# Two sets of eviction buffers and an earlier history copy in the up-projection of a streaming encoder layer

## The chip, the cores and the metric

The kernel runs on one core of a Trainium2 chip. The metric is device time in microseconds of one execution. Three executions of the kernel before took 2345.95, 2350.46 and 2352.51 us; the median is 2350.46. A fourth execution was profiled; all rows shown are from it.

## The reference

One layer of a hybrid encoder runs over 2048 prompt tokens and 8 sample streams of 16 tokens (17 tiles of 128 tokens in all). A head mixer (mLSTM and sliding-window attention) and an output projection come first; their result, normalised, is h. Then the part that the change touches:

```python
def conv_ffn(h, conv_prev, w_up, w_conv, b_conv, w_down):
    T = h.shape[1]
    u = h @ w_up                                   # 1024 -> 2 * 2816
    ext = jnp.concatenate([conv_prev.astype(u.dtype), u], axis=1)
    c = b_conv + sum(ext[:, j:j + T] * w_conv[j] for j in range(CONV_W))   # CONV_W = 3, causal
    a, g = jnp.split(c, 2, axis=-1)
    return (jax.nn.silu(g) * a) @ w_down, ext[:, -(CONV_W - 1):]
```

The convolution needs the two rows of u before the first one of its stretch: its history. For the prompt it starts at zero and runs on from block to block of tokens; each sample stream brings its own two rows (`state_conv`). The last two rows are outputs too.

## The kernel before, in words

**Stages.** Input projection with the mixer woven into it, output projection, up-projection (`f_ups`, about 934 to 1876 us of the profiled span), down-projection (`f_downs`). The up-projection works on three blocks of tokens (`FBLOCKS`: 6, 6 and 5 tiles, that is 768, 768 and 640 columns; the sample tile is the last of the third block), and in each block on 22 units j. A unit is 128 value rows and 128 gate rows of u, all tokens of the block.

**A unit.** Value and gate, first and second half of the tokens make four quarters. They are computed with seven half-size products instead of eight, and combinations of weights and of tokens are prepared for that (the steps are numbered 1 to 7). Each product is 12 matmuls of 128 rows (`f_product`, L1875): inputs are split into a high and a low part (`split`: the cast of the high part on ACT is L220, the subtraction of the low part on DVE is L221) and three of the four part products are taken. The order in which products run is written by hand and is the only order that is fixed (`ORDER`; engine PE alone is scheduled by hand): for unit j products 6, 2, 5, then 1 of unit j+1, 3 of j, 7 of j+1, 4 of j. Units alternate between two sets of three PSUM banks A, B, C; B takes products 6, 5 and 3 one on top of the other, A takes 1 and 2, C takes 7 and 4.

**Evictions** (`f_after`) follow the products. After 1, ACT copies bank A to B (L1888). After 6, ACT copies B to the tile u2 (L1900). After 2, ACT copies A into the tile u (L1902). After 5, ACT copies B to the tile u4 (L1904) and DVE adds C and u4 into u (L1905, for the sample tile L1907). After 3, ACT copies B into u (L1909, L1911). After 4, DVE adds C and u2 into u (L1914). A later product that adds to a bank waits until the eviction before it has read the bank: product 5 for L1900, product 3 for L1904, product 4 for L1905 and L1907.

**Convolution.** After product 4 the history is put in: POOL copies two columns of `prev` to the front of u (L1915) and, in the third block, two columns of each sample stream from `sconv` into u (L1917). Then, for value and for gate, ACT computes the last tap with the bias into the tile cc (L1921) and DVE adds the two other taps (L1923, two instructions for each). POOL saves the last two columns of u for the next block (L1924) and for the outputs (L1926). The first block's cc go to DRAM (L1929) and are read back (L1938) beside the later blocks; the gate is ACT's L1945 and DVE's L1946 and L1947; its result goes out by L1948 and L1950.

**Buffers.** Tiles come from pools on the left or right side of SBUF. A tile with a tag and `bufs=n` rotates over n places; writing a place again waits until its last readers are done. Before, u, u2 and u4 have one place each, cc has two. `skew` allocates an unused tile so that the pool after it starts where wanted.

**Order.** On ACT, DVE, POOL and SP a planner places each instruction by its own estimate of when it can start; every engine then works through its list in order, and an instruction that has to wait holds up those behind it. SP issues the transfers in the same way: raw weights (L1777, L1779, L1781), prepared weights that were kept (L1808 reads, L1815 writes), and from the end of the up-projection on the down-projection's weights (L2010) and inputs (L1992). Weights are prepared 6 to 8 products ahead (`AHEAD`). When a block of tokens ends, the next block's combinations are made and split on ACT and DVE (`f_tokens`, L1753 to L1759 and the split's tiles hh and hl); that is the change of block.

Of the kernel before, what the change touches and what calls it, by code (L numbers as in the profile page):

```python
# [8 lines left out]
F32 = mybir.dt.float32  # L9
# [5 lines left out]
P = 128  # L15
# [3 lines left out]
DB = 8  # L19
# [185 lines left out]
class Prog:  # L205
# [23 lines left out]
    def run(self):  # L229
        PS = bass.MemoryType.PSUM  # L230
        nb = len(OBLOCKS)
        with ExitStack() as es:
            def enter(*a, **k):
                cm = self.pool(*a, **k)
                return cm.__enter__(), cm
            close = lambda cm: cm.__exit__(None, None, None)
            self.cp = es.enter_context(self.pool("const"))
            self.dp = es.enter_context(self.pool("dram", space=bass.MemoryType.DRAM))
            es.enter_context(self.tc.manual_schedule(engines={mybir.EngineType.PE}))
            self.setup()  # L240
            self.wp = es.enter_context(self.pool("wsb"))
            self.dps = es.enter_context(self.pool("dps", 3, PS))
            self.tp, tcm = enter("tsb", side="right")
            self.tps, tpcm = enter("tps", 5, PS)
            self.xp, xcm = enter("xsb")
            self.mp, mcm = enter("isb")
            chains = Chains(self)
            self.xs, self.gates, self.i_done = {}, {}, 0
            self.i_begin()
            self.warm_up()  # L250
            chains.weave(self.i_dense())
            close(mcm)
            wx, wxcm = enter("wx1sb")
            self.skew(wx, 64)
            self.unit_more(wx)
            self.mp, mcm = enter("osb")
            self.o_setup()
            for b in range(nb - 1):
                chains.weave(self.late_done(self.o_block(b)))
            chains.until(NPT - 1)  # L260
            chains.drain()
            close(tpcm)
            close(tcm)
            self.fp, fcm = enter("fsb", side="right")
            self.fup, fpcm = enter("fup", 3, PS)
            self.f_setup()
            dense = self.o_block(nb - 1)
            first = self.f_hT(0)
            next(first)
            n = 0  # L270
            for i, _ in enumerate(dense):
                if i >= 8:
                    next(first, None)
                if i == 21:
                    self.f_tokens(0, 1, "t1", "t3", 7, "t2", 6)

                if i >= 22 and n < (2, 4, 5)[min((i - 22) // 4, 2)]:
                    self.f_next()
                    n += 1
            for _ in first:  # L280
                pass
            assert not self.norms
            close(mcm)
            close(wxcm)
            close(xcm)

            self.wx, wxcm = enter("wx2sb")
            self.skew(self.wx, 64)
            self.f2, f2cm = enter("f2sb")
            self.f3, f3cm = enter("f3sb")  # L290
            self.f_ups(n)
            self.skew(self.f2, 480)
            self.skew(self.wx, 448)
            close(f3cm)
            close(f2cm)
            self.f2, f2cm = enter("dsb")
            self.f_downs()
            for cm in (f2cm, wxcm, fpcm, fcm):
                close(cm)
# [1577 lines left out]
    def f_after(self, b, j, s):  # L1877

        nc, f2 = self.nc, self.f2
        V, S = nc.vector, nc.scalar  # L1880
        W = len(FBLOCKS[b]) * P
        h = W // 2
        has_s = NPT in FBLOCKS[b]
        WP = W - P if has_s else W
        n = WP + (DB * (DS + 2) if has_s else 0)
        A, B, C = [x[:, :h] for x in self.banks[j % 2]]
        if s == 1:
            S.copy(B, A)  # L1888
            return
        if s == 7:  # L1890
            return
        if s == 6:
            u = f2.tile([P, 2, 770], F32, name="u", tag="u", bufs=1)
            self.u = u, *[f2.tile([P, 384], F32, name=m, tag=m, bufs=1)[:, :h] for m in ("u2", "u4")]
        u, u2, u4 = self.u
        us = u[:, :, 2 + WP:2 + n].rearrange("p v (b l) -> p v b l", b=DB) if has_s else None
        m = WP - h
        dec = lambda z: z[:, m:].rearrange("p (b l) -> p b l", b=DB)
        if s == 6:
            S.copy(u2, B)  # L1900
        elif s == 2:
            S.copy(u[:, 0, 2:2 + h], A)  # L1902
        elif s == 5:
            S.copy(u4, B)  # L1904
            V.tensor_add(u[:, 1, 2 + h:2 + WP], C[:, :m], u4[:, :m])  # L1905
            if has_s:
                V.tensor_add(us[:, 1, :, 2:], dec(C), dec(u4))  # L1907
        elif s == 3:
            S.copy(u[:, 0, 2 + h:2 + WP], B[:, :m])  # L1909
            if has_s:  # L1910
                S.copy(us[:, 0, :, 2:], dec(B))  # L1911
        if s != 4:
            return
        V.tensor_add(u[:, 1, 2:2 + h], C, u2)  # L1914
        nc.gpsimd.tensor_copy(u[:, :, 0:2], self.prev[:, :, j])  # L1915
        if has_s:
            nc.gpsimd.tensor_copy(us[:, :, :, 0:2], self.sconv[:, :, j])  # L1917
        c = self.f3.tile([P, 2, 768], F32, name="cc", tag="cc", bufs=2)[:, :, :n]
        for v in range(2):
            w = [self.cw[:, v * NFF + j, i:i + 1] for i in range(4)]  # L1920
            S.activation(c[:, v], u[:, v, 2:2 + n], AF.Identity, bias=w[3], scale=w[2])  # L1921
            for i in (1, 0):
                V.scalar_tensor_tensor(c[:, v], u[:, v, i:i + n], w[i], c[:, v], op0=ALU.mult, op1=ALU.add)  # L1923
        nc.gpsimd.tensor_copy(self.prev[:, :, j], u[:, :, WP:WP + 2])  # L1924
        if has_s:
            nc.gpsimd.tensor_copy(self.convs[:, :, j], us[:, :, :, DS:])  # L1926
        if b == 0:

            nc.sync.dma_start(self.zc[j], c)  # L1929
            return  # L1930
        self.f_gate(c, b, j, WP, n)

        i = (b - 1) * NFF + j
        i = i if i < 18 else i - 6 if 24 <= i < 28 else None
        if b and i is not None:
            W0 = len(FBLOCKS[0]) * P
            c = self.f3.tile([P, 2, 768], F32, name="cc", tag="cc", bufs=2)[:, :, :W0]
            nc.sync.dma_start(c, self.zc[i])  # L1938
            self.f_gate(c, 0, i, W0, W0)
# [231 lines left out]
```

## Time and profile before

| | |
|---|---|
| median of three executions | 2350.46 us |
| the profiled execution's own time | 2345.55 us |
| its span, from first to last instruction | 2343.8 us |
| busy in the span: PE (matmuls) | 2304.7 us |
| PEld (weight loads) | 2116.7 us |
| DVE | 1805.6 us |
| ACT | 1298.6 us |
| POOL | 244.7 us |
| mean granted clock of PE | 0.996 |

PE stands for TensorE's matmuls, PEld for its weight loads, DVE for VectorE, ACT for ScalarE, POOL for GpSimd, SP (with "q" for its queue) for the engine that issues transfers. A row of a timeline has its start, its duration, engine, line, operation, the tiles written and read, the shape, the count, and in brackets the idle time before it with what ended that. A row of waits has the waiting engine, tile and line, then who ended the wait, the total in us, how many times, and the longest. A row of windows has the window, its length, and the busy time and count of each engine, then the granted clock, the share of DMA engines busy, and GB/s.

### The profile page before, as it was taken

The numbers are of one execution on the slowest core, as the hardware profiler recorded it, in microseconds if no ns is written. First come the engines' busy times: TensorE is split into PE (matmuls) and PEld (weight loads), VectorE is DVE, ScalarE is ACT, GpSimd is POOL, SyncE is SP. The second block draws the span as 40 slices with busy tenths as digits, with TensorE's granted clock in tenths as the row PEclk, the third lists the DMA queues.
The fourth block names the chain that finished last, engine by engine and source line by source line (L and its number), as shares of the span: only waits on it lengthen the run. The fifth ranks groups of instructions, "written<-read, shape, count | busy, mean of one in ns | idle before, by whom it ended". The sixth has DMA issues, their size and how long they took to land.

```text
span 2343.8 us, 39880 instructions
## 1 busy us (share of the span) xinstructions
PE 2304.7 (98%) x14425; PEld 2116.7 (90%) x14425; DVE 1805.6 (77%) x3150; ACT 1298.6 (55%) x2465; POOL 244.7 (10%) x298
## 2 busy tenths in 40 slices
PE   8999999999999999999999999999999999999998
PEld 8989998999987777999999999999999978888887
DVE  8676586797688888987888777768766776796897
ACT  5353466676666665555556555545544544654653
POOL 0101101101112221300001000002000100000100
PEclk9999999999999999999999999999999999999999
DMA  8888889889877667787777889878988776756753
GB/s 277 285 306 287 290 280 319 283 280 340 296 256 246 215 206 268 269 323 275 279 270 252 309 314 320 303 272 264 316 289 261 241 278 212 237 193 222 238 184 108
DMA packets 297365, 624.98 MB, mean 267 GB/s; under 512 B 47052, under 2 KB 140240, under 8 KB 297168
## 3 DMA queue, kind: packets, MB, share of 16 engines
q1 hardware_dynamic: 296304, 619.29, 77.6%
q10 hardware_dynamic: 864, 3.15, 0.4%
q8 instruction: 114, 1.87, 0.3%
q14 instruction: 83, 0.68, 0.1%
HBM read 451.78 MB, written 170.56 MB: 266 GB/s over the span
## 4 chain that ended last, share of the span: by engine, by line
PE 72%; DVE 6%; DMA 2%; issue 2%; ACT 2%; POOL 0%; SPq 0%; DVEq 0%; ACTq 0%; POOLq 0%
PE fup L1875 18%; PE dps L1875 18%; PE dps L2079 6%; PE dps L734 6%; PE fup L2079 6%; PE fht L2079 5%; PE dps L225 2%; PE dps L227 2%; PE dps L226 2%; PE ppo L1370 1%; PE psc L1321 1%; PE ppt L1364 1%; PE dps L759 1%; DVE hl L221 1%; DVE w L221 1%
## 5 line engine op out<-in xcount | busy, mean ns | idle before, releaser
L1875 PE MATMUL dps<-hh,uw 128*128 128x384 f32 (+1 forms) x1848 | 480.6, 328 | 6.8 <-ACT u L1900 1.9
L1875 PE MATMUL fup<-hh,uw 128*128 128x384 f32 (+1 forms) x1848 | 479.4, 328 | 2.8 <-ACT u L1900 2.7
L1875 PEld LDWEIGHTS dps<-hh,uw 128*128 128x128 f32 x1848 | 329.7, 188 | 11.0 <-ACT u L1900 3.0
L1923 DVE SCALAR_TENSOR_TENSOR cc<-u,cw,cc 128x768 f32<-128x768 f32 (+1 forms) x264 | 252.4, 977 | 107.7 <-ACT cc L1921 105.5
L1875 PEld LDWEIGHTS fup<-hh,uw 128*128 128x128 f32 x1848 | 329.8, 188 | 4.3 <-ACT u L1900 3.8
L1875 PE MATMUL fup<-hl,uw 128*128 128x384 f32 (+1 forms) x924 | 302.4, 327 | 0.5 <-DVE hl L221 0.5
L1875 PE MATMUL dps<-hl,uw 128*128 128x384 f32 (+1 forms) x924 | 302.0, 327 | 0.0
L734 PE MATMUL dps<-w,oh 128*128 128x256 f32 x1344 | 258.0, 286 | 4.1 <-ACT zev L800 2.7
L221 DVE TENSOR_TENSOR w<-wraw,w 128x1024 fp32r<-128x1024 f32 (+2 forms) x163 | 188.1, 1159 | 61.7 <-ACT w L220 60.6
L220 ACT CAST w<-wraw 128x1024 fp32r<-128x1024 f32 (+2 forms) x163 | 160.9, 993 | 122.6 <-PE dps L734 56.1
L734 PEld LDWEIGHTS dps<-w,oh 128*128 128x128 f32 x1344 | 213.0, 190 | 16.3 <-issue 8.9
L220 ACT CAST uw<-wraw 128x1024 fp32r<-128x1024 f32 x126 | 122.8, 977 | 184.2 <-PE dps L2079 106.4
L1921 ACT ACTIVATE cc<-u,cw 128x768 f32<-128x768 f32 (+1 forms) x132 | 129.5, 997 | 122.2 <-DVE u L1914 61.1
L221 DVE TENSOR_TENSOR uw<-wraw,uw 128x1024 fp32r<-128x1024 f32 x126 | 142.4, 1131 | 67.7 <-ACT uw L220 67.1
L734 PE MATMUL dps<-w,ol 128*128 128x256 f32 x672 | 189.1, 281 | 0.0
L734 PE MATMUL dps<-oh,w 128*128 128x256 f32 x896 | 168.8, 284 | 7.0 <-ACT oh L579 2.2
L1875 PEld LDWEIGHTS fup<-hl,uw 128*128 128x128 f32 x924 | 173.4, 188 | 1.3 <-DVE hl L221 1.3
L2079 PE MATMUL fup<-uw,fu 128*128 128x512 f32 x726 | 172.1, 393 | 1.7 <-DVE uw L221 1.7
L1875 PEld LDWEIGHTS dps<-hl,uw 128*128 128x128 f32 x924 | 173.4, 188 | 0.0
L2079 PEld LDWEIGHTS fup<-uw,fu 128*128 128x128 f32 x726 | 136.2, 188 | 33.1 <-DVE uw L221 2.2
L2079 PE MATMUL dps<-uw,fu 128*128 128x512 f32 x660 | 163.2, 393 | 0.0
L734 PEld LDWEIGHTS dps<-oh,w 128*128 128x128 f32 x896 | 140.7, 189 | 13.8 <-issue 4.1
(337 smaller groups left out, 4624.4 us busy)
## 6 DMA issues: line engine op xcount, KB each, us to landing
uw<-zw SPq DMA_DIRECT2D x176, 512.0 KB, 5.0
zw<-uw SPq DMA_DIRECT2D x88, 512.0 KB, 2.9
w<-zws SPq DMA_DIRECT2D x72, 512.0 KB, 6.6
wv<-wup SPq DMA_DIRECT2D x66, 512.0 KB, 5.8
wraw<-wi SPq DMA_DIRECT2D x64, 512.0 KB, 5.1
wraw<-zt SPq DMA_DIRECT2D x60, 512.0 KB, 4.1
wraw<-wdn SPq DMA_DIRECT2D x45, 512.0 KB, 3.9
wraw<-wo SPq DMA_DIRECT2D x40, 512.0 KB, 4.9
```

Of the source, the lines that this page charges most:

```text
L220: nc.scalar.copy(hi, src)
L221: nc.vector.tensor_sub(lo, src, hi.bitcast(F32))
L225: mm(out, ah, bh, start=start, stop=False)
L226: mm(out, ah, bl, start=False, stop=False)
L227: mm(out, al, bh, start=False, stop=stop)
L734: mm(o, l, r, start=s in (1, 7) and c == k == i == 0, stop=k == 3 and i == 2, skip_group_check=True)
L759: mm(o, x, w, start=k == i == 0, stop=k == KD - 1 and i == 2, skip_group_check=True)
L1321: nc.tensor.matmul(ps[kvh][:, j, :nk], q[rs, j0 + j], k[rs, sel], start=i == 0, stop=i == 2)
L1875: mm(ps, l[:, k], r[:, k], start=s in (1, 7) and k == 0 and i == 0, stop=k == 3 and i == 2, skip_group_check=True)
L1921: S.activation(c[:, v], u[:, v, 2:2 + n], AF.Identity, bias=w[3], scale=w[2])
L1923: V.scalar_tensor_tensor(c[:, v], u[:, v, i:i + n], w[i], c[:, v], op0=ALU.mult, op1=ALU.add)
L2079: mm(ps, l[:, k, c], r[:, k], start=s in (1, 4, 7) and u == 0 and k == 0 and i == 0, stop=u == nu - 1 and k == n - 1 and i == 2, skip_grou ...
```

## The change

The tiles u, u2 and u4 get two places each (`bufs=2`). The history copies L1915 and L1917 are issued when the unit's tiles are taken, after product 6, and no longer after product 4; what they copy is the same. To make room, the scratch that is kept at the bottom of SBUF for transfers issued by POOL is set to 2048 bytes a partition; without the argument the program's constants begin at address 16384, with it at 2048, so all that is allocated from the left lies 14336 bytes lower. The padding after f2's pool is 448 bytes instead of 480, so that the pool behind it starts at the same place modulo 512. Lines behind the insertion have numbers up to 3 higher in the changed kernel (L1900, L1902, L1904, L1905 and L1914 become L1903, L1905, L1907, L1908 and L1917); L1915 and L1917 become L1895 and L1897; from L1918 on the numbers agree again. Line numbers in the prediction are those of before.

```diff
             self.f_ups(n)
-            self.skew(self.f2, 480)
+            self.skew(self.f2, 448)
             self.skew(self.wx, 448)
...
         if s == 6:
-            u = f2.tile([P, 2, 770], F32, name="u", tag="u", bufs=1)
-            self.u = u, *[f2.tile([P, 384], F32, name=m, tag=m, bufs=1)[:, :h] for m in ("u2", "u4")]
+            u = f2.tile([P, 2, 770], F32, name="u", tag="u", bufs=2)
+            self.u = u, *[f2.tile([P, 384], F32, name=m, tag=m, bufs=2)[:, :h] for m in ("u2", "u4")]
+            nc.gpsimd.tensor_copy(u[:, :, 0:2], self.prev[:, :, j])
+            if has_s:
+                nc.gpsimd.tensor_copy(u[:, :, 2 + WP:2 + n].rearrange("p v (b l) -> p v b l", b=DB)[:, :, :, 0:2], self.sconv[:, :, j])
...
         V.tensor_add(u[:, 1, 2:2 + h], C, u2)
-        nc.gpsimd.tensor_copy(u[:, :, 0:2], self.prev[:, :, j])
-        if has_s:
-            nc.gpsimd.tensor_copy(us[:, :, :, 0:2], self.sconv[:, :, j])
         c = self.f3.tile([P, 2, 768], F32, name="cc", tag="cc", bufs=2)[:, :, :n]
...
-    nc = bacc.Bacc("TRN2", target_bir_lowering=False, num_devices=1)
+    nc = bacc.Bacc("TRN2", target_bir_lowering=False, num_devices=1, dynamic_dma_scratch_size=2048)
```

## The prediction

> **What bounds the kernel now.** I read the page's busy shares first, then busy time in windows over the up-projection (about 934 to 1876 us), then what TensorE's weight loads and matmuls waited for there, then the timelines at the places found. The page:
>
> ```profile
> span 2343.8 us, 39880 instructions
> PE 2304.7 (98%) x14425; PEld 2116.7 (90%) x14425; DVE 1805.6 (77%) x3150; ACT 1298.6 (55%) x2465; POOL 244.7 (10%) x298
> ```
>
> TensorE is the bound: the whole program leaves its matmuls only 39 us of idle time. The windows below show where the up-projection's share lies; columns are the window, its length, then busy time and instruction count of PE, PEld, DVE, ACT, POOL.
>
> ```profile
> 1250.00:1280.00 30.00, 27.55 (x158) 26.91 (x157) 28.39 (x25) 20.20 (x26) 3.94 (x3) 1.00 0.68 231
> 1280.00:1580.00 300.00, 300.00 (x1737) 298.96 (x1737) 212.61 (x261) 154.53 (x252) 14.76 (x41) 1.00 0.87 303
> 1580.00:1610.00 30.00, 27.49 (x168) 26.93 (x168) 29.00 (x29) 19.57 (x28) 10.87 (x3) 1.00 0.66 210
> 1650.00:1660.00 10.00, 9.26 (x62) 8.84 (x61) 6.29 (x10) 4.70 (x9) 0.86 (x3) 1.00 0.90 298
> 1660.00:1855.00 195.00, 194.61 (x1322) 193.56 (x1322) 128.72 (x195) 96.98 (x191) 17.10 (x63) 1.00 0.88 280
> 1855.00:1880.00 25.00, 23.08 (x150) 21.75 (x149) 22.92 (x31) 17.40 (x28) 5.48 (x8) 1.00 0.62 187
> ```
>
> Inside a block of tokens (second row) PE does not stop at all. It stops where one block gives way to the next (first and third row), once at 1656, and at the end (last row). At the two changes of block DVE is busy 28.4 and 29.0 of 30 us. Who ended the stops, from 930 to 1925 us (total, times, longest):
>
> ```profile
> PEld fup L1875 <- ACT u L1900: 3.8, 4, 1.5
> PEld dps L1875 <- ACT u L1900: 3.0, 4, 1.6
> ...
> PEld dps L1875 <- DVE u L1905: 2.0, 1, 2.0
> PEld dps L1875 <- DVE u L1907: 1.5, 2, 1.1
> PEld dps L1875 <- ACT u L1904: 1.3, 3, 0.8
> PEld fup L1875 <- ACT u L1904: 0.5, 2, 0.4
> PE fup L1875 <- ACT u L1900: 2.7, 3, 1.2
> PE dps L1875 <- ACT u L1900: 1.9, 2, 1.3
> ```
>
> Four lines that evict quarters (L1900, L1904, L1905, L1907) hold PE up for 12.1 us by weight loads; L1900, the copy of bank B after product 6, is the largest with 6.8 (4.6 by matmuls). A stop costs something between its two views, so I take the mean of matmul idle and weight-load idle in a window. That bounds everything the change can reach: 2.8 + 2.8 + 0.95 + 0.9 + 2.6 = 10 us over the five windows with stops.
>
> **The change, part by part** (line numbers of before).
>
> *Two buffers for u, u2, u4.* No instruction is added or removed. What the single u holds back today is mostly not PE:
>
> ```profile
>   DVE cc L1923: 13.9, 12
>   ACT cc L1921: 40.9, 21
> ```
>
> The first row is L1902's idle time on ACT until the last convolution step of the unit before has read u: 1.2 us in each of 12 units. The second is who waited for L1917, the sample history's copy: L1921, in 21 of 22 units, 40.9 us of ACT. Both waits go (L1917 is dealt with below). Their worth on PE is zero inside a block, where PE is 300.00 of 300 busy; if that cover were gone the 54.8 us would be the price, which no window supports, since PE's whole idle time there is under 0.5 us per 195 or 300. What remains is the order in which ACT takes its work, and I went through the built order of both programs. PE's order is unchanged; ACT's, DVE's and SP's differ from the first change of block on.
>
> First change of block, ACT (start, duration):
>
> ```profile
> 1258.05 0.62 ACT L220 CAST uw<-wv 128x512 fp32r<-128x512 f32 x1 [3.55 <-PE dps L1875]
> 1258.58 1.48 ACT L220 CAST hh<-hraw 128x1536 fp32r<-128x1536 f32 x1
> 1259.96 1.02 ACT L1921 ACTIVATE cc<-u,cw 128x768 f32<-128x768 f32 x1
> 1260.89 0.45 ACT L1900 COPY u<-dps 128x384 f32<-128x384 f32 x1
> 1274.25 0.63 ACT L220 CAST uw<-wv 128x512 fp32r<-128x512 f32 x1
> 1276.01 1.03 ACT L1921 ACTIVATE cc<-u,cw 128x768 f32<-128x768 f32 x1 [1.13 <-DVE u L1914]
> 1276.95 0.46 ACT L1900 COPY u<-fup 128x384 f32<-128x384 f32 x1
> ```
>
> L1900 stands behind the old unit's second L1921, which waits for DVE (L1914, 1.13 us at the second place). With a second u2 it needs only product 6, and the changed order has it ahead of all three rows: possible from about 1258.05 instead of 1260.89, and from 1274.25 instead of 1276.95. Both leads (2.8 and 2.7 us) exceed the longest stop (1.6), so both stops go: 30 minus 27.55 is 2.45, 30 minus 26.91 is 3.09, mean **-2.8 us**. Next to be late is DVE: 1.6 us of its 30 are idle there, and the casts of tokens moved behind L1900 come 0.45 us later each time. If DVE ends the stops instead, this term is nearer 0; I take all of it because the stops now end with ACT, not DVE.
>
> Second change of block: 2.51 and 3.07, mean 2.8. Of it L1905 has 2.0 by weight loads and DVE's order at L1905 is the same after; that stays. The rest is L1900, again moved ahead of L1921: **-0.9 us**.
>
> At 1656 ACT itself waits for a transfer:
>
> ```profile
> 1653.96 1.76 ACT L1921 ACTIVATE cc<-u,cw 128x656 f32<-128x656 f32 x2 [3.23 <-DMA zf<-cc]
> 1655.63 0.40 ACT L1900 COPY u<-fup 128x320 f32<-128x320 f32 x1
> ```
>
> L1900 stays behind both L1921 there, and cc keeps its two buffers. The stop is 0.74 to 1.16; a gate (L1945) that moves one cast forward may bring that transfer forward. I take a third: **-0.3 us**.
>
> Inside the third block (0.39 to 1.44 idle, mean 0.9) the stops belong to L1904 and L1907, and a unit there looks like this:
>
> ```profile
> 1737.39 0.27 ACT L1911 COPY u<-fup 128x128 f32<-128x128 f32 x1
> 1738.93 0.62 ACT L220 CAST uw<-wv 128x512 fp32r<-128x512 f32 x1 [1.27 <-PE dps L1875]
> 1741.50 1.76 ACT L1921 ACTIVATE cc<-u,cw 128x656 f32<-128x656 f32 x2 [1.95 <-POOL u L1917]
> 1743.16 0.40 ACT L1900 COPY u<-dps 128x320 f32<-128x320 f32 x1
> 1740.70 0.49 DVE L1914 TENSOR_TENSOR u<-fup,u 128x320 f32<-128x320 f32 x1 [0.42 <-PE fup L1875]
> ```
>
> *The history's copies moved to the unit's beginning.* 66 copies L1915 and 22 copies L1917 stay on POOL, one place earlier, no DMA among them. L1915 of a unit now goes ahead of the save L1924 of the unit before, and waits for the same last L1923 two units back as today; L1924 queues behind it, and only the same unit's L1915 in the next block and u's release wait for L1924, a unit or more later: 0 us. L1917 no longer waits for L1914, so the value half of L1921 can run at 1737.7 instead of 1741.5. DVE then takes two L1923 before L1914, which goes back by about 0.3 us; the gate half ends, and L1900 with it, about 0.6 us sooner; L1945 and L1904 behind it gain more. The window's **-0.9 us** goes.
>
> The last window has 1.92 to 3.25 idle, mean 2.6. By the same laying out of queues L1900 comes 0.5 us sooner, but L1904 now stands behind the down-projection's cast of a weight group and L1945; I take **-0.6 us**.
>
> *Scratch and paddings.* Scratch for POOL's own DMAs shrinks, so everything allocated from the left moves down 14336 bytes; nearly all left-hand tiles keep their address modulo 512. POOL issues no DMA: every queue of the page is hardware or instruction. u2, u4 and one u move by 32 bytes modulo 64. L1902 (u) and L1900 (u2) are now 32 apart and take 463 and 459 ns at the median:
>
> ```profile
> L1902 ACT COPY u<-fup x33: 407/463/489, 943.4 to 1857.3; 128x384 f32<-128x384 f32 x22, 128x320 f32<-128x320 f32 x11
> L1900 ACT COPY u<-fup x33: 401/459/484, 942.5 to 1854.0; 128x384 f32<-128x384 f32 x22, 128x320 f32<-128x320 f32 x11
> ```
>
> 4 ns times 264 copies is 1 us on ACT, beside PE: 0.
>
> **Sum**: -2.8 - 0.9 - 0.3 - 0.9 - 0.6 = -5.5 us, between 0 and -10. The profiled execution took 2345.55 us, 4.9 below the median 2350.46 of the three runs; the mean of all four is 2348.6. I put the sum on that mean: **2343 us**, 7.4 below the median.
>
> **The rivals.** (1) *All stops at evictions go*: -10 us, also L1905's, because ACT hands it u4 sooner. Against it: DVE is 29.0 of 30 busy there. 2338.6. (2) *Nothing reaches PE*: DVE becomes the releaser at both changes of block; for it, its 1.0 to 1.6 us of idle time; against it, that L1900 is the named releaser. 2348.6. (3) *POOL gets in DVE's way.* The sample copies take 212 ns at the median but up to 1141:
>
> ```profile
> L1917 POOL COPY u<-sconv x22: 212/214/1141, 1615.5 to 1875.9; 128x32 f32<-128x32 f32 x22
> L1915 POOL COPY u<-prev x66: 188/494/12615, 937.4 to 1870.2; 128x4 f32<-128x4 f32 x66
> ```
>
> and L1915 from 188 to 12615, so POOL is held back while DVE works. Moved beside L1915, the 22 copies meet a working DVE. Charged in full, 22 times 0.214 is 4.7 us: 2347.8. DVE has 66 of 195 us idle in that block, so I take 0. The Trainium skill ("SBUF — State Buffer", section Who interferes with whom) says that a DVE instruction with two SBUF inputs and a GpSimd read exclude each other for a whole instruction and whoever starts first wins; the stretched L1915 agrees, and the rule speaks against the move. By the rule with POOL always first the sum would be -0.8, by the rows -5.5.
>
> (4) *Slower: a raw weight load falls behind in SP's queue.* In the third block the built order puts the load of wv behind one more L1808, which waits for PE:
>
> ```profile
> 1740.30 0.33 SPq L1777 DMA_DIRECT2D wv<-wup  x1
> 1751.24 0.62 ACT L220 CAST uw<-wv 128x512 fp32r<-128x512 f32 x1 [1.27 <-PE fup L1875]
> wv<-wup SPq DMA_DIRECT2D x15, 512.0 KB, 5.9
> SPq L1808 <- PE dps L1875: 100.1, 57, 3.8
> ```
>
> It is issued at 1740.30, lands 5.9 later at 1746.2, and the next cast from a wv is at 1751.24: 5.0 us in hand at least, against one wait of at most 3.8. If two waits add, a unit is late by up to 2.6; over 20 units 52 us, 2395 at worst. It decides from 0.6 us a unit (12.5 us, 2355.6); since each unit's load could catch up I price it there.
>
> **How the numbers follow.** 0.3% of the median is 7 us, about what a measurement of this kernel can tell from no change: under 2343.4 is faster. Forecast 0.62, its own range 2338 to 2348, split 0.33 faster and 0.29 same; rival 1 0.12 (faster); rival 2 0.08 and rival 3 0.04 (same); rival 4 0.14 (slower). Together 0.45, 0.41, 0.14. The range goes from all of it on the lowest run (2345.55 - 10 = 2335.5, and 1 below) to rival 4's point of decision, a little under: 2334.5 to 2355.
>
> **What would show it.** Right: in 1250 to 1280 PE's idle time falls from 2.45 to under 0.5 and L1900 as releaser from 6.8 to under 3; L1902 no longer waits for L1923, nor L1921 for POOL; PE's and DVE's busy times stay. Wrong: L1923, hl or L1905 in L1900's place with equal totals (rival 2), a longer L1923 in the third block (rival 3), or L220 waiting for wv's transfer in many units (rival 4). A change before 930 us, where every engine's order is unchanged, would mean that addresses matter, which no row here prices.

## The result, and the profile after

The changed kernel takes 2344.69 us at the median of 20 executions (2340.11 to 2350.57); the kernel before, beside it, takes 2349.06 us (2344.25 to 2355.42). The ratio is 0.9982 with a 95% interval of 0.9975 to 0.9989: 4.2 us less (2.6 to 5.9). That is inside the 0.3% that the prediction called no change, and on the side it forecast. The time, 1.7 us above the 2343 of the forecast, came out of parts that were not those of the forecast. The rest is about that. In the experiments below one of the 12 executions of e3_hist took 10117 us and one of the 12 of e9_load11 9955 us; the medians given there count them, the ratios leave them out.

The page of the changed kernel, its two first lines:

```profile
span 2340.1 us, 39886 instructions
PE 2301.8 (98%) x14425; PEld 2115.6 (90%) x14425; DVE 1806.9 (77%) x3150; ACT 1302.5 (56%) x2465; POOL 249.6 (11%) x298
```

The work is the same on every engine, and TensorE (PE) is still the bound. The windows that the prediction looked at, now of the changed kernel, with the beginning of the down-projection as a seventh; the columns are the window, its length, busy time and count of PE, PEld, DVE, ACT and POOL, granted clock, DMA share, GB/s:

```profile
1250.00:1280.00 30.00, 29.20 (x169) 28.88 (x168) 28.41 (x25) 20.69 (x27) 10.24 (x3) 1.00 0.70 233
1280.00:1580.00 300.00, 300.00 (x1737) 299.28 (x1736) 213.67 (x262) 156.45 (x253) 16.30 (x42) 1.00 0.88 305
1580.00:1610.00 30.00, 28.26 (x178) 27.96 (x177) 29.73 (x33) 20.08 (x30) 11.81 (x7) 1.00 0.68 212
1650.00:1660.00 10.00, 10.00 (x71) 10.00 (x70) 7.39 (x12) 5.41 (x11) 1.34 (x4) 1.00 0.94 288
1660.00:1855.00 195.00, 190.72 (x1296) 189.67 (x1296) 129.08 (x191) 98.54 (x188) 17.29 (x62) 1.00 0.88 279
1855.00:1880.00 25.00, 23.89 (x155) 22.75 (x155) 22.84 (x31) 18.01 (x30) 2.44 (x6) 1.00 0.62 193
1880.00:1925.00 45.00, 45.00 (x197) 36.51 (x196) 34.80 (x39) 19.26 (x25) 0.00 (x0) 1.00 0.86 310
```

The last of these windows in the kernel before, which the prediction did not show:

```profile
1880.00:1925.00 45.00, 43.26 (x189) 34.94 (x188) 33.43 (x37) 19.36 (x25) 0.00 (x0) 1.00 0.87 315
```

PE's idle time falls from 2.45 to 0.80 us at the first change of block, from 2.51 to 1.74 at the second, from 0.74 to 0 at 1656. In the third block (fifth row) it rises from 0.39 to 4.28. In the down-projection, of which the prediction says nothing, 1.74 us go.

Who ended the stops of PE in the changed kernel, from 930 to 1925 us (waits of PE: total, times, longest):

```profile
PE dps L1875 <- ACT u L1907: 2.8, 2, 1.7
PE dps L1875 <- DVE u L1908: 2.5, 2, 1.7
PE fup L1875 <- DVE hl L221: 1.5, 2, 1.2
PE fup L1875 <- ACT u L1903: 1.3, 1, 1.3
PE dps L1875 <- ACT uw L220: 1.4, 2, 0.7
PE dps L1875 <- ACT u L1903: 1.3, 2, 1.0
```

L1903, the copy of bank B after product 6 (L1900 before), is down from 4.6 to 2.6 us. What is left of it and the larger stop of L1907 are all in the third block or at the end, where the kernel before had 1.3 us in two stops of the one and 0.5 us in one of the other.

Windows cut a stage at fixed times. To compare executions I took the start of the first matmul of certain products from each trace, and the differences between them. The change of block runs from product 1 of unit 21 of the old block to product 7 of unit 1 of the new one; "units 3 to 8" from product 7 of unit 3 to product 7 of unit 9; the first unit ends where its product 5 begins. The changed kernel was profiled twice. All in us:

| stretch | before | after | after, second profile |
|---|---|---|---|
| all ahead of the up-projection | 933.95 | 933.25 | 931.03 |
| first unit | 9.71 | 10.71 | 10.61 |
| rest of the first block | 303.76 | 303.45 | 303.64 |
| first change of block | 36.39 | 34.48 | 34.46 |
| second block | 293.24 | 293.10 | 293.89 |
| second change of block | 34.17 | 33.12 | 33.11 |
| units 1 to 2 of the third block | 24.62 | 24.62 | 24.62 |
| units 3 to 8 | 76.51 | 79.21 | 78.46 |
| units 9 to 19 | 135.42 | 135.42 | 135.42 |
| end of the up-projection | 27.50 | 26.18 | 26.18 |
| down-projection | 468.49 | 466.54 | 466.54 |

Five rows carry the change: -1.9, -1.05, +2.7 (+1.95 in the second profile), -1.3 and -1.95. Their sum is -3.5 (-4.3), and the time changed by -4.2. The first two rows of the table and the second block vary between executions of one program: by 3.9, 1.0 and 0.9 us between the two profiles of e2_bufs below.

### The profile page after: what moved, and what is told of

Same layout as the page of the kernel before. It is cut to its first block, busy times and chain, and to the rows that moved or that the text cites. A ratio compares the mean times of both kernels' runs of the same rounds, so it can differ in the third digit from the quotient of the medians.

```text
span 2340.1 us, 39886 instructions
## 1 busy us (share of the span) xinstructions
PE 2301.8 (98%) x14425; PEld 2115.6 (90%) x14425; DVE 1806.9 (77%) x3150; ACT 1302.5 (56%) x2465; POOL 249.6 (11%) x298
## 5 line engine op out<-in xcount | busy, mean ns | idle before, releaser
L1923 DVE SCALAR_TENSOR_TENSOR cc<-u,cw,cc 128x768 f32<-128x768 f32 (+1 forms) x264 | 257.7, 978 | 124.0 <-ACT cc L1921 105.4
L221 DVE TENSOR_TENSOR w<-wraw,w 128x1024 fp32r<-128x1024 f32 (+2 forms) x163 | 187.8, 1157 | 59.3 <-ACT w L220 58.2
L220 ACT CAST w<-wraw 128x1024 fp32r<-128x1024 f32 (+2 forms) x163 | 161.0, 993 | 122.3 <-PE dps L734 63.8
L220 ACT CAST uw<-wraw 128x1024 fp32r<-128x1024 f32 x126 | 122.7, 977 | 180.8 <-PE dps L2079 106.4
L1921 ACT ACTIVATE cc<-u,cw 128x768 f32<-128x768 f32 (+1 forms) x132 | 131.9, 999 | 118.2 <-DVE u L1917 96.4
L221 DVE TENSOR_TENSOR uw<-wraw,uw 128x1024 fp32r<-128x1024 f32 x126 | 142.6, 1132 | 68.1 <-ACT uw L220 67.7
```

Source lines behind the costliest of these rows:

```text
L220: nc.scalar.copy(hi, src)
L221: nc.vector.tensor_sub(lo, src, hi.bitcast(F32))
```

## The experiments

Theory at this point: the buffers give the two changes of block; something about transfers costs the third block; the down-projection gains by accident of an order. Rivals: the lower addresses do it (scratch); the history's move does it all; the third block's loss is rival 4's late weight load.

**Placement alone, buffers alone, history alone, and a third cc.** The first four kernels split the change into its parts, and add one buffer to it. Edits are against the changed kernel unless it is said otherwise, and each ratio is to executions of the kernel before taken beside that kernel's.

e1_space, the kernel before with the smaller scratch and nothing else:

```diff
-    nc = bacc.Bacc("TRN2", target_bir_lowering=False, num_devices=1)
+    nc = bacc.Bacc("TRN2", target_bir_lowering=False, num_devices=1, dynamic_dma_scratch_size=2048)
```

> Placement alone: the kernel before with the scratch at 2048 bytes, everything on the left 14336 bytes lower, every engine's order as before. If placement carries part of the gain (theory P): ratio 0.9985 or less, and the stop of 1.7 us at 1918 us goes here too. If it is the buffers' doing (theory B): ratio 1.000 within 0.07%, idle time of PE in 1250 to 1280 stays at 2.4 us and in 1580 to 1610 at 2.5, and what differs outside the up-projection is chance.

Measured: 2348.3 us, ratio 0.9996 (0.9985 to 1.0006). The stretches of the table are those of before (36.39, 34.18, 76.03, 27.51, 468.49; the 0.5 us at units 3 to 8 is within what two profiles of one program differ by there). No effect of the addresses is seen, as the prediction took it.

e2_bufs, the buffers with the history where it was:

```diff
             u = f2.tile([P, 2, 770], F32, name="u", tag="u", bufs=2)
             self.u = u, *[f2.tile([P, 384], F32, name=m, tag=m, bufs=2)[:, :h] for m in ("u2", "u4")]
-            nc.gpsimd.tensor_copy(u[:, :, 0:2], self.prev[:, :, j])
-            if has_s:
-                nc.gpsimd.tensor_copy(u[:, :, 2 + WP:2 + n].rearrange("p v (b l) -> p v b l", b=DB)[:, :, :, 0:2], self.sconv[:, :, j])
...
         V.tensor_add(u[:, 1, 2:2 + h], C, u2)
+        nc.gpsimd.tensor_copy(u[:, :, 0:2], self.prev[:, :, j])
+        if has_s:
+            nc.gpsimd.tensor_copy(us[:, :, :, 0:2], self.sconv[:, :, j])
```

> Two buffers each, history still copied after product 4. Theory B (the second buffers let the planner put L1900 ahead of L1921 at the changes of block): PE's idle time falls to about 0.8 in 1250 to 1280 and 1.7 in 1580 to 1610 as in the changed kernel. Theory H (the earlier history copy moves the third block's convolution forward, into transfers of cc that have not landed, and costs the 4 us in units 5 to 8): no such stops here, PE idle in 1660 to 1855 at 0.4 to 1, so ratio 0.9965 to 0.998, lower than the full change's 0.9982. If H is wrong and the buffers make those stops: idle about 4 there, ratio about 0.998 or above.

Measured: 2341.69 us, ratio 0.9971 (0.9960 to 0.9983). The changes of block take 34.51 and 33.12, as after; units 3 to 8 take 76.91 (76.92 in a second profile), as before; the end of the up-projection 26.62; the down-projection 468.50, as before. So the buffers give the whole of both changes of block. Its interval overlaps the changed kernel's; which of the two is faster is not settled by that. These stretches add up to 3.3 us under before, a little less than the 4.0 us at which the interval begins; no profile shows where more could come from.

e3_hist, the history moved with one buffer each:

```diff
-            self.skew(self.f2, 448)
+            self.skew(self.f2, 480)
...
-            u = f2.tile([P, 2, 770], F32, name="u", tag="u", bufs=2)
-            self.u = u, *[f2.tile([P, 384], F32, name=m, tag=m, bufs=2)[:, :h] for m in ("u2", "u4")]
+            u = f2.tile([P, 2, 770], F32, name="u", tag="u", bufs=1)
+            self.u = u, *[f2.tile([P, 384], F32, name=m, tag=m, bufs=1)[:, :h] for m in ("u2", "u4")]
```

> One buffer each, history copied when the unit begins. Theory B: PE idle in 1250 to 1280 and 1580 to 1610 as before (2.4 and 2.5). Theory H: L1921 no longer waits for L1917 and the stops in units 5 to 8 of the third block appear, 2 to 4 us in 1660 to 1855; ratio 0.9995 to 1.0015. If the history's move is what helps: ratio 0.998 to 0.999.

Measured: 2344.41 us, ratio 0.9983 (0.9972 to 0.9994). The changes of block are those of before (36.41, 34.18), units 3 to 8 take 76.82, the end 26.49, the down-projection 466.52, as after. The history's move gives the down-projection's 1.95 us, which no part of the prediction touches. Neither part alone costs the third block anything that shows beside the 76.0 to 77.4 us of the kernels with the order of before (e1 and e9 below); together they do. The theory H of these two expectations, that the history's move brings the loss by itself, fails with that.

e4_cc3, the changed kernel with three buffers for cc:

```diff
-        c = self.f3.tile([P, 2, 768], F32, name="cc", tag="cc", bufs=2)[:, :, :n]
+        c = self.f3.tile([P, 2, 768], F32, name="cc", tag="cc", bufs=3)[:, :, :n]
...
-            c = self.f3.tile([P, 2, 768], F32, name="cc", tag="cc", bufs=2)[:, :, :W0]
+            c = self.f3.tile([P, 2, 768], F32, name="cc", tag="cc", bufs=3)[:, :, :W0]
...
-    nc = bacc.Bacc("TRN2", target_bir_lowering=False, num_devices=1, dynamic_dma_scratch_size=2048)
+    nc = bacc.Bacc("TRN2", target_bir_lowering=False, num_devices=1, dynamic_dma_scratch_size=1024)
```

> The changed kernel with three buffers for cc (scratch 1024 for the room). Theory H (units 5 to 8 stop because ACT waits for cc's transfers): PE idle in 1660 to 1855 falls from 4.3 to under 1, L1921 no longer waits for the store of zf, ratio 0.996 to 0.997 (4 us under the changed kernel). If the raw weights' load in SP's queue is what stops those units: idle stays at 2 or more and L220 still waits for wv; ratio 0.998.

Measured: 2339.86 us (six executions, 2338.82 to 2342.38), ratio 0.9960 (0.9945 to 0.9974): faster than both kernels. Units 3 to 8 fall from 79.21 to 74.31, 2.2 under before; every other stretch is the changed kernel's.

What the third cc takes away is seen in the ACT timeline. First the changed kernel in unit 5 of the third block (start, duration, then the row; in brackets the idle time before it and who ended it):

```profile
1657.25 0.85 ACT L1945 ACTIVATE th<-cc 128x768 f32<-128x768 f32 x1 [1.07 <-DMA cc<-zc]
...
1661.33 0.94 ACT L1921 ACTIVATE cc<-u,cw 128x656 f32<-128x656 f32 x1 [2.34 <-DMA zf<-cc]
1662.17 0.60 ACT L220 CAST uw<-wv 128x512 fp32r<-128x512 f32 x1
1664.25 0.94 ACT L1921 ACTIVATE cc<-u,cw 128x656 f32<-128x656 f32 x1 [1.47 <-DVE u L1917]
1665.09 0.41 ACT L1903 COPY u<-dps 128x320 f32<-128x320 f32 x1
```

Then the same unit with three cc:

```profile
1657.53 0.85 ACT L1945 ACTIVATE th<-cc 128x768 f32<-128x768 f32 x1 [0.73 <-DVE cc L1947]
...
1660.46 0.94 ACT L1921 ACTIVATE cc<-u,cw 128x656 f32<-128x656 f32 x1
1661.65 0.62 ACT L220 CAST uw<-wv 128x512 fp32r<-128x512 f32 x1 [0.25 <-PE dps L1875]
1664.31 0.94 ACT L1921 ACTIVATE cc<-u,cw 128x656 f32<-128x656 f32 x1 [2.04 <-DVE u L1917]
1665.17 0.43 ACT L1903 COPY u<-dps 128x320 f32<-128x320 f32 x1
```

ACT works through its list in order. With two cc, L1921 waits until a convolution result has left for memory (zf<-cc), L1945 until a convolution result of the first block has come back from it (cc<-zc); with three, neither waits for a transfer, and PE's stops at L1903 go. The waits of ACT for these transfers from 1640 to 1720 us, in the changed kernel:

```profile
ACT cc L1921 <- DMA zf<-cc: 6.2, 4, 2.4
ACT th L1945 <- DMA cc<-zc: 4.0, 3, 1.7
ACT uw L220 <- DMA wv<-wup: 2.5, 2, 2.2
```

and with three cc the one row of that kind that is left:

```profile
ACT uw L220 <- DMA wv<-wup: 2.9, 3, 1.5
```

The third row of the changed kernel is rival 4's wait for a raw weight load. It remains with three cc at 2.9 us, and units 3 to 8 take 74.31 us there, with one stop of 0.2 us. So rival 4's wait is there, and is not what costs the time; the kernel before has more of it (4.0 us in 2 from 1640 to 1760 us).

**Which buffer, whose cc, which gates.** e5_u2u4_only is the changed kernel with one u; e6_u_only has one u2 and one u4.

```diff
-            self.skew(self.f2, 448)
+            self.skew(self.f2, 480)
...
-            u = f2.tile([P, 2, 770], F32, name="u", tag="u", bufs=2)
+            u = f2.tile([P, 2, 770], F32, name="u", tag="u", bufs=1)
```

> The changed kernel with one buffer for u, and two each for u2 and u4 as in the change. Theory A (the prediction's: the copy of bank B waits for the old unit's u2, so a second u2 is what lets it go ahead): the first change of block takes 34.5 us as after (before 36.4), the second 33.1 (before 34.2), and the time is that of the changed kernel, 2342 to 2346. Rival B (the copies of bank A into u are what holds the order; u2 comes along behind): 36.4 and 34.2 as before, and 2345 to 2348. In both the down-projection keeps the 466.5 us of the changed kernel, since the history is copied early.

```diff
-            self.u = u, *[f2.tile([P, 384], F32, name=m, tag=m, bufs=2)[:, :h] for m in ("u2", "u4")]
+            self.u = u, *[f2.tile([P, 384], F32, name=m, tag=m, bufs=1)[:, :h] for m in ("u2", "u4")]
```

> The changed kernel with two buffers for u alone, and one each for u2 and u4. Theory A (a second u2 is what counts): both changes of block as before the change, 36.4 and 34.2 us, and 2345 to 2348. Rival B (a second u counts): 34.5 and 33.1, and 2342 to 2346. If each does part of it, the first change lies between at about 35.5.

Measured: e5 2342.81 us, 0.9975 (0.9962 to 0.9988), changes of block 34.51 and 33.12, units 3 to 8 78.30. e6 2347.11 us, 0.9997 (0.9986 to 1.0008), changes of block 38.72 and 34.17, units 3 to 8 76.53. Waits of PE from 1250 to 1300 us, e5:

```profile
PE dps L1875 <- DVE u L1908: 0.8, 1, 0.8
```

and e6:

```profile
PE fup L1875 <- ACT u L1903: 1.9, 1, 1.9
PE dps L1875 <- ACT u L1903: 1.3, 1, 1.3
```

Theory A holds: u2 and u4 are what lets L1903 go ahead, and the larger tile u needs no second place. (0.8 of e6's 38.72 is a longer stop; the other 1.6 are a dip of the clock, below.) The 13.9 us that ACT waited for L1923 before, which a second u was to remove, were indeed worth nothing. The third block's loss goes with u2 and u4 too: both kernels copy the history early, and only e5 has most of the loss.

e7_cc3_alone, the third cc in the kernel before (edit against that kernel, with the smaller scratch for room, as in e1):

```diff
-        c = self.f3.tile([P, 2, 768], F32, name="cc", tag="cc", bufs=2)[:, :, :n]
+        c = self.f3.tile([P, 2, 768], F32, name="cc", tag="cc", bufs=3)[:, :, :n]
...
-            c = self.f3.tile([P, 2, 768], F32, name="cc", tag="cc", bufs=2)[:, :, :W0]
+            c = self.f3.tile([P, 2, 768], F32, name="cc", tag="cc", bufs=3)[:, :, :W0]
```

> The kernel before with a third buffer for cc, and nothing of the change. Theory A (ScalarE waits for transfers of cc in the third block whatever the change does, and the change only brings more work behind these waits): units 3 to 8 of the third block take about 74.3 us (before 76.5, after 79.2); the changes of block stay 36.4 and 34.2, the down-projection 468.5; time about 2 us under before, 2346 to 2348. Rival B (the third buffer helps only together with the change): units 3 to 8 stay at 76.5, and 2348 to 2351.

Measured: 2347.18 us, ratio 0.9989 (0.9973 to 1.0005); units 3 to 8 at 74.43, all else as before (36.42, 34.17, 468.48). The transfers held PE up in the kernel before too, by 2.1 us; the change made that 4.8 (with three cc 74.4, with two 76.5 before and 79.2 after).

e8_gates_later, the changed kernel with the four read-backs that fell into units 2 to 5 of the third block done in units 8 to 11:

```diff
-        i = i if i < 18 else i - 6 if 24 <= i < 28 else None
+        i = i if i < 18 else i - 12 if 30 <= i < 34 else None
```

> The changed kernel with the four gates of the first block that are read back from memory done six units later, in units 8 to 11 of the third block in place of 2 to 5. Theory A (the stops of units 3 to 8 come from these read-backs, which meet the weights and the sums zf in the queues while cc has two buffers): units 3 to 8 fall from 79.2 us to 74.5 to 76.5, units 9 to 20 grow from 135.4 to 136 or more, and the time is 2340 to 2344. Rival B (zf's transfers and wv's load alone make them): units 3 to 8 stay within 1 us of 79.2.

Measured: 2342.5 us, ratio 0.9971 (0.9959 to 0.9983). Units 3 to 8 fall to 73.86 and units 9 to 19 grow from 135.42 to 137.78, with one stop of 1.3 us at L1903 there. In the place that they left, PE does not stop at all. The stops follow the read-backs, as theory A has it; in the later place they cost 2.4 us where they cost 4.9 to 5.3 in the changed kernel.

**The down-projection.** The eleventh load of raw weights (L2010) is what differs there. SP's queue and ACT of the kernel before:

```profile
1906.23 1.63 SPq L2010 DMA_DIRECT2D wraw<-wdn  x2
```

```profile
1914.75 1.57 ACT L220 CAST uw<-wraw 128x1024 fp32r<-128x1024 f32 x2 [1.54 <-DMA wraw<-wdn]
```

and PE behind it:

```profile
1918.46 2.80 PE L2079 MATMUL fup<-uw,fu 128*128 128x512 f32 x11 [1.74 <-DVE uw L221]
```

In the changed kernel:

```profile
1885.71 0.37 SPq L2010 DMA_DIRECT2D wraw<-wdn  x1
1886.72 1.38 SPq L1992 DMA_DIRECT2D r<-zf  x3
```

```profile
1899.29 1.04 ACT L220 CAST uw<-wraw 128x1024 fp32r<-128x1024 f32 x1
```

The load's place in SBUF is free 12.15 us after the up-projection's end in both. The built order of the changed kernel has it ahead of the inputs r<-zf (L1992), and it is issued at 12.18 us after that end; the order of before has it behind them, at 30.95. There it lands at 39.44, ACT and DVE prepare it late, and PE stops for 1.74 us. In the other profiles the two go together as well: 466.5 us with the load issued at about 12 us in all kernels with the early history, 468.5 with the late load in e1, e2 and e7. e9_load11 tests it by itself: the kernel before, with a place of its own for this one load (edit against that kernel).

```diff
-        raw = self.wp.tile([P, 1024], F32, name="wraw", tag="wraw", bufs=4)
+        raw = self.wp.tile([P, 1024], F32, name="wraw", **({"tag": "wraw11", "bufs": 1} if self.nw == 11 else {"tag": "wraw", "bufs": 4}))
...
-    nc = bacc.Bacc("TRN2", target_bir_lowering=False, num_devices=1)
+    nc = bacc.Bacc("TRN2", target_bir_lowering=False, num_devices=1, dynamic_dma_scratch_size=2048)
```

> The kernel before, with a place of its own in SBUF for the eleventh raw weight load of the down-projection (and the smaller scratch to make room for it), so that this load no longer waits for a place and stands early in SP's queue instead of behind the loads r<-zf. Nothing of the change is in it. Theory A (the down-projection's 1.95 us come from this one load's place in the queue): the down-projection takes 466.5 us (before 468.5), DVE's stop of 1.74 us near the 42nd us of that stage is gone, all other stages are those of before within 0.3 us (units 3 to 8 of the third block within 1), and the time is about 2 us under before. Rival B (the history's copies or what comes with them do it in another way, and the load only moved along): 468.5 as before.

Measured: 2346.14 us, ratio 0.9990 (0.9979 to 1.0000). The first change of block took 38.34 us in its profile, 2 over before, 1.6 of it by the clock (below), and units 3 to 8 took 77.41, 0.9 over; neither is part of the edit. The load does not take the changed kernel's place at 12 us of the stage: nothing holds it, and SP issues it in the input projection already.

```profile
68.36 0.43 SPq L2010 DMA_DIRECT2D wraw<-wdn  x1
```

The down-projection takes 466.49 us; the window of its beginning shows PE without a stop:

```profile
1876.00:1925.00 49.00, 49.00 (x225) 40.43 (x224) 36.80 (x42) 21.33 (x28) 1.28 (x2) 1.00 0.83 296
```

So the 1.95 us are the lateness of this load, which in the kernel before stands behind the inputs in SP's queue. That the planner's estimates moved it there when the history moved is what the two built orders show; which estimate tipped it was not traced.

**Second profiles.** Two kernels were profiled again, to see whether the third block's stops belong to the order of work or to how transfers fall.

> The changed kernel once more, for a second profile. If the stops in units 3 to 8 of the third block are a property of its order of work, that stretch takes 78.0 us or more again (first profile 79.2, before 76.5) with stops at the same products (5 of unit 5, 5 of unit 6, 3 of unit 7); if they hang on how the transfers happen to fall, it takes 75 to 78 and the stops are at other products. The other stages are within 0.3 us of the first profile, the first unit of the up-projection excepted.

> The buffers without the history's move once more, for a second profile. If the stretch of units 3 to 8 belongs to the order of work it takes 76.5 to 77.3 us again (first profile 76.9) with stops at product 5 of units 4 and 6; if it is how the transfers fall, it differs by over 1 us from that.

Measured: 78.46 and 76.92 us for units 3 to 8. The totals repeat within 0.8 us, the places less so: the changed kernel stopped at product 5 of units 5, 6 and 7 and product 3 of unit 7 in the first profile (1.0, 1.3, 0.3 and 1.7 us), at product 5 of units 4 and 5 and product 3 of unit 7 in the second (0.6, 2.1 and 1.0). With one order of work ACT waited for transfers of cc 7 times in the first profile (10.2 us, 1640 to 1760 us) and 5 times in the second (9.1 us); which transfer is late varies.

## Why the prediction was right or wrong

The time and its direction came out within 2 us, and this was partly luck. One term was right, two had the right sign and the wrong size, the two for the third block had the wrong sign, and a term of nearly 2 us was missing.

- *First change of block, -2.8.* Mis-sized: -1.9. The mechanism was right: a second u2 lets the copy after product 6 go ahead of L1921 (e5 against e6), and both of L1900's stops go. But a stop of 0.80 us comes in its place, by DVE. This is rival 2 in small: the prediction named DVE as the next to be late, with 1.6 us of idle time in 30, and then took all of the term because the stops ended with ACT. The copy (L1903) now stands ahead of the casts and of L1921, at the time that the prediction named (1258.05):

```profile
1258.04 0.48 ACT L1903 COPY u<-dps 128x384 f32<-128x384 f32 x1 [3.55 <-PE dps L1875]
1258.41 1.49 ACT L220 CAST hh<-hraw 128x1536 fp32r<-128x1536 f32 x1
1259.79 1.04 ACT L1921 ACTIVATE cc<-u,cw 128x768 f32<-128x768 f32 x1
```

and the stop that is left:

```profile
1269.27 0.45 PE L1875 MATMUL dps<-hh,uw 128*128 128x384 f32 x1 [0.80 <-DVE u L1908]
```

- *Second change of block, -0.9, L1905's part stays.* Right: -1.05 (2.8 less 2.0, as the prediction has it, is 0.8 and not 0.9), and the stop of 1.74 us that is left is ended by DVE's L1908, the former L1905.
- *At 1656, -0.3, and in the third block, -0.9.* The step that failed. It said: "The gate half ends, and L1900 with it, about 0.6 us sooner; L1945 and L1904 behind it gain more. The window's -0.9 us goes." Measured over units 3 to 8, where 1656 lies too, is +2.7 (+1.95) against these -1.2. The step laid out ACT's queue by what the compute engines release, and read the one wait for a transfer (3.23 us for zf<-cc, quoted by the prediction) as a local event. That wait was a sign that cc with its two buffers is short in that stretch: a third one gains 2.1 us in the kernel before too (e7). With buffers and early history together the waits for transfers of cc grow there, from 5.0 us in 2 (3.2 for zf<-cc, 1.8 for cc<-zc, 1640 to 1760 us) to 10.2 in 7, and L1903 and L1907 are behind them. The third cc (e4, e7) and the moved read-backs (e8) both take the loss away. Each part alone raises the waits as well (e2 8.9 us in 4 and 7.2 in 3, e3 7.2 in 4) without a loss that shows in units 3 to 8. ACT also waits for zf<-cc in the second block, in the kernel before 16.5 us in 11, where PE does not stop. So such a wait costs only where what stands behind it has no time in hand; where that point lies for each part is not settled.
- *End of the up-projection, -0.6.* Right in sign, mis-sized: -1.3, of which each part alone has most (e2 -0.9, e3 -1.0; they do not add up).
- *The down-projection.* Missing: -1.95. The prediction says that the orders of ACT, DVE and SP differ from the first change of block on, and follows them to 1880 us only. (In the traces ACT's order differs from 957 us on, in the first block, where the stretch stays at 303.8 and 303.5 us.) The difference was there to be read: one load that stands ahead of the inputs and not behind them.
- *Two waits of ACT worth nothing.* Right. They did go: the copy after product 2 (L1902, L1905 in the changed kernel) now waits for PE alone, and L1921 no longer for POOL. But L1921 now waits elsewhere; in the changed kernel (930 to 1880 us):

```profile
ACT cc L1921 <- DVE u L1917: 96.4, 60, 2.8
```

and in the kernel before:

```profile
ACT cc L1921 <- DVE u L1914: 61.1, 41, 2.8
ACT cc L1921 <- POOL u L1917: 40.9, 21, 3.1
```

  L1917 of the one and L1914 of the other are the same addition after product 4. 102.0 us became 96.4: the copy had been last of two releasers that are close together.
- *Scratch and paddings, 0.* Right (e1). *History's copies on POOL, 0.* Right: the 22 sample copies, in the changed kernel,

```profile
L1897 POOL COPY u<-sconv x22: 207/210/217, 1596.6 to 1855.1; 128x32 f32<-128x32 f32 x22
```

  have a maximum of 217 ns where it was 1141. Rival 3 had them meet a working DVE in the new place and hold it; DVE's busy time is 1806.9 us against 1805.6. The traces show why not. In the kernel before three of the 22 copies began while DVE ran L221 (at 1691.31, 1864.83 and 1875.87 us); they took 610, 880 and 1141 ns and ended less than 0.1 us after that L221, and the other 19, all of 212 to 218 ns, met no instruction of DVE. In the changed kernel L1895 goes just ahead of L1897 on POOL and takes that wait (493 ns at the median of its 66, 183 at the least), so that L1897 begins when it is over. The three copies agree with the Trainium skill's page "SBUF — State Buffer" (section Who interferes with whom), by which a DVE instruction with two inputs in SBUF and a GpSimd instruction that reads SBUF shut each other out.
- *Rival 1* (all stops go) fails on L1908. *Rival 4* fails: L220 waits for a raw weight load no more than before (2.5 us in 2 against 4.0 in 2, 1640 to 1760 us), and not in each unit.

## What to carry to other kernels

A buffer that frees an in-order engine from one wait lets it run into the next one sooner, so the list to go through before the change is everything that this engine waits for behind that point, transfers first: here the third buffer belonged to cc, and with it the kernel takes 2339.86 us. Where a planner writes the orders, compare both built orders to the end of the program and price every transfer that changes its place, also in stages that the change doesn't name. When a forecast of several small terms hits the total, check the terms one by one; here about 4.8 us of error one way (4.1 by the second profile) met 2.8 the other way.

## What the runs showed of the hardware that was not expected

PE's clock can drop to half for 3.4 us after a stop of less than 2 us. In e8 PE restarts at 1601.72 after the stop of 1.74 us at the second change of block; these are its rows:

```profile
1601.72 0.45 PE L1875 MATMUL dps<-hh,uw 128*128 128x384 f32 x1 [1.74 <-DVE u L1908]
1602.01 0.39 PE L1875 MATMUL dps<-hl,uw 128*128 128x384 f32 x1
1602.20 0.84 PE L1875 MATMUL dps<-hh,uw 128*128 128x384 f32 x2
...
1605.40 0.39 PE L1875 MATMUL fup<-hh,uw 128*128 128x320 f32 x1
```

From 1602.20 to 1605.40 ten starts follow at 320 ns each, where the same matmuls of the changed kernel follow at 173 or 174; the granted clock of 1600 to 1606 us is 0.72:

```profile
1600.00:1606.00 6.00, 4.28 (x16) 4.27 (x17) 6.00 (x7) 2.17 (x4) 5.59 (x3) 0.72 0.38 147
```

The stretch is 1.6 us longer for it (34.70 against 33.12). The same followed a stop of 1.9 us in e6 (1282.76) and one of 1.85 in e9 (1260.59), at the first change of block; the other profiles have the same stop of 1.70 to 1.74 us at the second change without it. So a stop of this length costs its own time, and in 3 of the 13 profiles of this case, once each in the up-projection, about as much again.

Length is not all: after_again stopped for 2.12 us at 1664 us and kept its clock. The traces' records of the granted clock change on a grid of 3.41 us, whose position differs between executions, and what counts is the idle time within one step of it. Over the up-projections of all 13 profiles PE was idle for more than 1.80 us of a step twice (1.92 in e6, 1.85 in e9), and both times the next step ran at half clock. Seven steps had 1.72 to 1.74 us, and one was followed by it (e8); none with 1.70 or less was. The 2.12 us of after_again lay across two steps, with 1.62 in the one. So the point lies near half a step, as far as these cases show.

The Trainium skill's page "TensorE: Matmul & The Clock Gate" (Part 1) has the array fall back to half its clock after an idle window of about 3.4 us whose position is not tied to the kernel; half speed, the length and the free position agree with that, but here a window that was idle for about half of its length was enough.

The time ahead of the up-projection, where all engines' orders are the same in all kernels but for the one load of e9, was 931.0 to 940.3 us. The granted clock of the first 400 us differs with it, though not in strict order; e1, the slowest:

```profile
0.00:400.00 400.00, 384.13 (x3118) 368.27 (x3119) 281.77 (x543) 198.04 (x379) 35.99 (x32) 0.97 0.85 288
```

and e2, one of the fastest (932.2):

```profile
0.00:400.00 400.00, 382.28 (x3170) 365.98 (x3171) 285.02 (x559) 203.32 (x393) 37.36 (x33) 1.00 0.86 293
```

52 matmuls more in the same 400 us. The spread of 9.3 us is more than any term of the change, so a single profile's span says little about a change of this size; 20 executions gave an interval 0.14% wide.
